# Storing the first row of the first tile by itself in a DMA-bound rotary-embedding kernel

## The chip, the cores and the metric

The kernel runs on 1 core of one Trainium2 chip. The metric is device time of one execution in microseconds (us). A profile covers one execution; its span is about 1.4 us shorter than the measured time of that execution. Only executions that were classed as fast enter comparisons.

## The reference, cut to what matters

```python
batch, seq, dim, num_heads = 16, 512, 1024, 16           # head_dim 64, half 32
x = x.reshape(batch, seq, num_heads, head_dim)
x1, x2 = x[..., :half_dim], x[..., half_dim:]
rotated = np.concatenate([x1 * cos - x2 * sin, x1 * sin + x2 * cos], axis=-1)   # float32
```

The input is 33.5 MB and so is the output, each moved once.

## The kernel before

Each of 128 partitions holds several sequence positions, called rows; a row is 1024 floats, 4 KB. A tile is one batch with 4 rows per partition (the first two and the last two tiles, 2 MB) or two batches with 8 rows (six tiles, 4 MB). Tiles are computed in place in a ring of 40 rows per partition: the first six loads fit at once, the last four wait until earlier tiles have been stored.

```python
RING = 5 * R2                     # R1 = 4, R2 = 8
LAG = 10                          # rows of work between a slot's last sum and the refill's issue
...
def stores_of(k):                 # stores that must land before slot k is loaded again
    return sum(b * R1 // R2 == k for b, _ in tiles)
...
def on_sync(sp):                  # all stores, queue q1
    for u in range(NU):
        t, r, k = where(u)
        if r == tiles[t][1] - 1:                      # last row of tile t is summed
            wait_added(sp, u)
            k = u // R2
            sp.dma_start(in_dram(o1, o2, t), in_sbuf(t)).then_inc(...)
...
# ScalarE: all loads, queue q10, and one kind of eviction, in one program order
for u in range(NU):
    if PE2[u]:
        ae.wait_ge(sem_e, n_pe[u])
        ae.activation(xs[:, u % RING, :], t1_ps[:, u % NT1, :], COPY).then_inc(sem_a, 1)
    for t in later.get(u, ()):
        ae.wait_ge(sem_out[k], 16 * stores_of(k))     # stands still until the stores have landed
        load(ae, t)
```

For each row GpSimd multiplies by the sine table, VectorE by the cosine table, and the two products are added by VectorE or by TensorE with ScalarE.

## Time and profile before

| | before |
|---|---|
| time, median of the first 3 runs | 161.40 us (161.40 to 161.44) |
| span of the profile | 159.8 us |
| bytes moved by DMA, mean rate | 67.26 MB, 421 GB/s |
| GpSimd, VectorE busy | 85%, 82% |
| load queue q10 + store queue q1, share of 16 engines | 49.8% + 48.8% |
| first store issued, last store issued, last store landed | 20.2, 151.1, 159.7 us |

How to read it: a share of a DMA queue is the time its packets took, divided by sixteen engines times the span. As both queues together take 98.6%, the sixteen DMA engines are the resource that is full.

### The profile page before, as it was taken

Reading aid. Unit: us, or ns where it says so; the run is one execution under the profiler, and the core shown is the slowest. Engines: PE = TensorE matmul, PEld = TensorE weight load, DVE = VectorE, ACT = ScalarE, POOL = GpSimd, SP = SyncE. Lnnn points to the kernel's source line nnn. Section 1 sums busy time; section 2 is a strip of 40 time slices with the busy share of each in tenths; the row PEclk is TensorE's granted clock in tenths of the full one; section 3 lists DMA queues with packets and bytes.
Section 4 is the critical chain, followed back from the end, with each engine's and each line's share of the span. In section 5 each row is a group of like instructions: output and inputs, shape, how many; then the busy total and the mean of one; then the engine's idle time right before and its main releaser. Section 6 shows DMA issues by size and latency. Waiting matters only on the chain.

```text
span 159.8 us, 568 instructions
## 1 busy us (share of the span) xinstructions
PE 70.9 (44%) x94; PEld 23.3 (15%) x94; DVE 130.6 (82%) x117; ACT 23.9 (15%) x26; POOL 136.4 (85%) x67
## 2 busy tenths in 40 slices
PE   6050005375437642680943409435848764950000
PEld 1020002021202210220211002110222121310000
DVE  0069998799999999987989729899989998989500
ACT  0320000205020502022012020222022202130000
POOL 5069999999999999999999999994999999289400
PEclk9999999959876995576598775995555555576555
DMA  5999999999999999999999999999999999999997
GB/s 144 395 458 480 394 394 431 422 509 410 394 427 427 494 418 402 451 459 404 402 468 443 394 459 451 402 435 418 418 439 472 435 402 418 492 402 435 390 447 304
DMA packets 3170, 67.26 MB, mean 421 GB/s; under 512 B 352, under 2 KB 608, under 8 KB 608
## 3 DMA queue, kind: packets, MB, share of 16 engines
q10 hardware_dynamic: 1728, 33.69, 49.8%
q1 hardware_dynamic: 1440, 33.56, 48.8%
q14 instruction: 2, 0.02, 0.0%
HBM read 33.69 MB, written 33.55 MB: 421 GB/s over the span
## 4 chain that ended last, share of the span: by engine, by line
DMA 30%; POOL 18%; issue 17%; DVE 17%; PE 8%; ACT 3%; ACTq 2%; POOLq 0%; DVEq 0%; SPq 0%
DMA out_dram<-x_sb 18%; POOL t_sb L265 18%; DMA x_sb<-in_x_dram 11%; DVE x_sb L312 8%; PE t_ps L220 8%; DVE t_ps L301 7%; ACT x_sb L186 3%; ACTq L153 1%; DVE t_sb L294 1%; ACTq L174 1%; POOLq L144 0%; POOLq L146 0%; DVEq L311 0%; DVEq L146 0%; SPq L137 0%
## 5 line engine op out<-in xcount | busy, mean ns | idle before, releaser
L265 POOL TENSOR_TENSOR t_sb<-x_sb,s_sb 128x1024 f32<-128x1024 f32 x58 | 134.1, 2363 | 12.5 <-ACT s_sb L178 6.5
L220 PE MATMUL t_ps<-t_sb,ident 128*128 128x512 f32 x84 | 66.1, 940 | 64.8 <-DVE t_ps L301 34.7
L301 DVE TENSOR_TENSOR t_ps<-x_sb,pair_ps 128x1024 f32<-128x1024 f32 x48 | 57.7, 1223 | 8.2 <-ACT x_sb L186 7.9
L312 DVE TENSOR_TENSOR x_sb<-t_ps,t_sb 128x1024 f32<-128x1024 f32 x43 | 52.4, 1220 | 2.7 <-POOL t_sb L265 2.6
L186 ACT ACTIVATE x_sb<-t_ps 128x1024 f32<-128x1024 f32 x21 | 21.5, 1023 | 109.8 <-PE t_ps L220 97.7
L220 PEld LDWEIGHTS t_ps<-t_sb,ident 128*128 128x128 f32 x84 | 21.4, 279 | 109.2 <-DVE t_ps L301 60.2
L301 DVE TENSOR_TENSOR t_ps<-x_sb,tab_ps 128x1024 f32<-128x1024 f32 x16 | 19.3, 1222 | 1.1 <-DMA x_sb<-in_x_dram 0.6
L294 DVE TENSOR_TENSOR t_sb<-x_sb,tab_ps 128x1024 f32<-128x1024 f32 x6 | 7.3, 1215 | 0.0
L272 DVE COPY tab_ps<-stage 128x128 f32<-128x128 f32 x1 | 0.3, 295 | 7.6 <-DMA stage<-in_cos_dram 7.6
L203 PE MATMUL pair_ps<-stage,pick 128*128 128x256 f32 x4 | 2.0, 668 | 5.1 <-DMA stage<-in_sin_dram 5.1
L196 PE MATMUL t_ps<-zero 128*128 128x512 bf16 x6 | 2.7, 630 | 1.3 <-DVE zero L270 1.3
L177 ACT ACT_TABLE_LOAD x1 | 1.3, 1283 | 5.4 <-issue 5.4
L203 PEld LDWEIGHTS pair_ps<-stage,pick 128*128 128x128 f32 x4 | 1.2, 326 | 6.1 <-issue 6.0
L246 POOL TENSOR_SCALAR_AFFINE_SELECT pick<-pick 128x128 f32<-128x128 f32 x2 | 1.4, 704 | 0.1
L196 PEld LDWEIGHTS t_ps<-zero 128*128 128x128 bf16 x6 | 0.7, 137 | 2.4 <-DVE zero L270 1.2
L270 DVE MEMSET zero<- 128x256 uint32 x1 | 0.3, 272 | 0.9 <-PEq L345 0.9
L177 ACT ACTIVATE s_sb<-stage 128x128 f32<-128x128 f32 x1 | 0.3, 310 | 2.3 <-DMA stage<-in_sin_dram 2.3
L181 ACT ACTIVATE s_sb<-pair_ps 128x256 f32<-128x256 f32 x1 | 0.4, 384 | 1.7 <-PE pair_ps L203 1.7
L231 POOL MEMSET ident<- 128x128 f32 x1 | 0.2, 205 | 0.3 <-POOLq L345 0.3
L182 ACT ACTIVATE s_sb<-pair_ps 128x256 f32<-128x256 f32 x1 | 0.4, 378 | 0.0
L233 POOL TENSOR_SCALAR_AFFINE_SELECT ident<-ident 128x128 f32<-128x128 f32 x1 | 0.3, 294 | 0.1
L345 POOL MEMSET const-float32-0.0<- 128x1 f32 x1 | 0.1, 98 | 0.3 <-issue 0.3
(7 smaller groups left out, 1.3 us busy)
## 6 DMA issues: line engine op xcount, KB each, us to landing
x_sb<-in_x_dram ACTq DMA_DIRECT2D x6, 4096.0 KB, 38.8
out_dram<-x_sb SPq DMA_DIRECT2D x6, 4096.0 KB, 25.7
x_sb<-in_x_dram ACTq DMA_DIRECT2D x4, 2048.0 KB, 22.7
out_dram<-x_sb SPq DMA_DIRECT2D x4, 2048.0 KB, 15.0
stage<-in_cos_dram ACTq DMA_DIRECT2D x1, 64.0 KB, 7.5
stage<-in_sin_dram ACTq DMA_DIRECT2D x1, 64.0 KB, 7.3
```

The costliest lines, as they stand in the source:

```text
L153: eng.dma_start(in_sbuf(t), in_dram(x1, x2, t)).then_inc(sem_in[t], 16)
L174: ae.dma_start(stage[:, i, :], table.rearrange("(s r) d -> s (r d)", r=R1)).then_inc(sem, 16)
L177: ae.activation(s1_sb[:, :, 0, :], sv, COPY, scale=-1.0)
L186: ae.activation(xs[:, u % RING, :], t1_ps[:, u % NT1, :], COPY).then_inc(sem_a, 1)
L196: pe.matmul(t1_ps[:, k, b * BANK:(b + 1) * BANK], zero[:, 0:P], zero[:], start=True, stop=True).then_inc(sem_w, 1)
L203: pe.matmul(pair_ps[:, k].rearrange("p c r d -> p (c r d)"), pick[:, k].rearrange("q s b -> q (s b)"), stage[:].rearrange("q c f -> q (c f)"),
L220: ins = pe.matmul(t1_ps[:, u % NT1, b * BANK:(b + 1) * BANK], ident[:], t2[:, b * BANK:(b + 1) * BANK], start=False, stop=True, skip_group ...
L246: pl.affine_select(out=pick[:, k], in_=pick[:, k], compare_op=mybir.AluOpType.is_equal, fill=0.0, base=-k, pattern=[[-2, P // 2], [0, 2]], ...
L265: pl.tensor_tensor(t2_sb[:, u % NT2, :, :, :], swapped(k), over_heads(s_of(t, r)), mult).then_inc(sem_p, 1)
L294: ve.tensor_tensor(t2_sb[:, u % NT2, :, :, :], swapped(k), over_heads(v_ps), mult)
L301: ve.tensor_tensor(t1_ps[:, u % NT1, :].rearrange("p (h d) -> p h d", d=HALF), x_sb[:, k, :, :, :].rearrange("p h t d -> p (h t) d"), c_of ...
L312: ve.tensor_tensor(xs[:, k, :], t1_ps[:, u % NT1, :], t2_sb[:, u % NT2, :, :, :].rearrange("p h t d -> p (h t d)"), add,).then_inc(sem_v, 1)
```

## The change

The intent is to let the store queue start some 7 us earlier: row 0 of the first tile is stored alone when it is summed, rows 1 to 3 follow in one transfer.

```diff
-        def in_dram(single, pairs, t):
+        def in_dram(single, pairs, t, r=0):
             b, n = tiles[t]
-            return single[b] if n == R1 else pairs[:, b:b + 2, :]
+            return single[b, :, r * dim:] if n == R1 else pairs[:, b:b + 2, :]
 ...                                             (in_sbuf likewise)
-            return sum(b * R1 // R2 == k for b, _ in tiles)
+            return (k == 0) + sum(b * R1 // R2 == k for b, _ in tiles)
 ...
+                if u == 0:
+                    wait_added(sp, u)
+                    sp.dma_start(o1[0, :, 0:dim], xs[:, 0, :]).then_inc(sem_out[0], 16)
                 if r == tiles[t][1] - 1:
                     wait_added(sp, u)
                     k = u // R2
-                    sp.dma_start(in_dram(o1, o2, t), in_sbuf(t)).then_inc(...)
+                    sp.dma_start(in_dram(o1, o2, t, t == 0), in_sbuf(t, t == 0)).then_inc(...)
```

More of the change, by code (lines that the diff above doesn't have):

```diff
@@ L111, in bass_split_heads_rope_kernel, with in_sbuf @@
         xs = x_sb[:].rearrange("p n h t d -> p n (h t d)")
-        def in_dram(single, pairs, t):
+        def in_dram(single, pairs, t, r=0):
             b, n = tiles[t]
-            return single[b] if n == R1 else pairs[:, b:b + 2, :]
-        def in_sbuf(t):
+            return single[b, :, r * dim:] if n == R1 else pairs[:, b:b + 2, :]
+        def in_sbuf(t, r=0):
             b, n = tiles[t]
             k = b * R1 % RING
-            return x_sb[:, k:k + n].rearrange("p n h t d -> p (n h t d)")
+            return x_sb[:, k + r:k + n].rearrange("p n h t d -> p (n h t d)")
         def where(u):
@@ L160, in on_sync @@
                     k = u // R2
-                    sp.dma_start(in_dram(o1, o2, t), in_sbuf(t)).then_inc(sem_out[k] if k < EARLY else sem_rest, 16)
+                    sp.dma_start(in_dram(o1, o2, t, t == 0), in_sbuf(t, t == 0)).then_inc(sem_out[k] if k < EARLY else sem_rest, 16)
             sp.wait_ge(sem_rest, 16 * sum(stores_of(k) for k in range(EARLY, NU // R2)))
```

## The prediction

> **What bounds the kernel now.** I read the strip of 40 slices on the profile page first, because it shows every engine and the transfers side by side; then the transfers by stage; then single stretches of two microseconds.
>
> ```profile
> DVE  0069998799999999987989729899989998989500
> POOL 5069999999999999999999999994999999289400
> DMA  5999999999999999999999999999999999999997
> DMA packets 3170, 67.26 MB, mean 421 GB/s; under 512 B 352, under 2 KB 608, under 8 KB 608
> q10 hardware_dynamic: 1728, 33.69, 49.8%
> q1 hardware_dynamic: 1440, 33.56, 48.8%
> ```
>
> GpSimd is 85% busy and VectorE 82%, with gaps near the end. The DMA row has none: 9 in every slice but the first and the last. Queue q10 carries the loads (issued by ScalarE), q1 the stores (issued by SyncE); together they take 98.6% of sixteen engines over the whole span. The next view divides the span into stretches; its last two columns are the DMA share and GB/s.
>
> ```profile
> 0.00:4.00 4.00, 2.74 (x6) 0.73 (x6) 0.27 (x1) 0.00 (x0) 2.33 (x9) 1.00 0.54 143
> 4.00:24.00 20.00, 2.05 (x4) 1.18 (x4) 14.64 (x14) 2.45 (x5) 14.44 (x7) 1.00 1.00 424
> 24.00:140.00 116.00, 64.07 (x82) 20.94 (x83) 106.26 (x95) 20.28 (x20) 110.41 (x48) 0.70 1.01 434
> 140.00:158.00 18.00, 2.05 (x3) 0.44 (x2) 9.43 (x8) 1.20 (x2) 9.27 (x4) 0.59 0.98 421
> 158.00:160.00 2.00, 0.00 (x0) 0.00 (x0) 0.00 (x0) 0.00 (x0) 0.00 (x0) 0.50 0.33 139
> ```
>
> Loads alone (4 to 24 us) move at 424 GB/s, loads and stores mixed at 434, stores alone (140 to 158 us) at 421. All three have full engines. The kernel is therefore a start of some 2.5 us without data, 67 MB at about 430 GB/s (156 us), and a tail of about 1 us: 159.8 us of span, 161.4 us measured.
>
> The chain that ended last seems to contradict this, since its last pieces before the final store are computation:
>
> ```profile
> 142.77 6.97 POOL t_sb L265 x3
> 149.75 0.03 issue
> 149.77 0.02 DVEq L311
> 149.79 0.04 issue
> 149.84 1.23 DVE x_sb L312
> ```
>
> The final store is issued at 151.14 and lands 8.6 us later. But the queue listing of 140 to 158 us has q1 alone at 98.0% of all engines: the store issued before it, at 143.14, lands only 11.8 us later, at 154.9. The final store waits in its queue for some 3.8 us and then takes 2.10 MB / 0.43 MB per us = 4.9 us: 159.8. So computation has about 3.8 us of slack at the end, and the transfers set it.
>
> **What the skill says.** "DMA: Bandwidth & Descriptors", section "Queues, rings and completion order", says that an engine goes round-robin between the queues that have work for it, a packet at a time. The trace agrees. In the two microseconds from 38 to 40 the listing by queue (packets, MB, share) is
>
> ```profile
> q10 hardware_dynamic: 16, 0.52, 60.6%
> q1 hardware_dynamic: 16, 0.26, 30.6%
> ```
>
> that is, each of 16 engines serves one load packet and one store packet in turn, although one is twice as large. The durations come out of it: 0.606 x 32 us / 16 = 1.21 us for the 32 KB row group of a load, 0.306 x 32 / 16 = 0.61 us for the 16 KB of a store. The same page, "Specifications", gives a fabric ceiling of 435 GB/s; the mixed stretch reaches 434. "Perfetto Trace Analysis", section "DMA Optimizations", says that splitting a DMA may finish the task sooner "If DMA engines are generally idle". That condition doesn't hold here: 98.6% busy. This is the heart of my prediction.
>
> **The change part by part.** On the compute engines nothing moves: the comparison of the instruction streams shows the same instructions in the same order on all but SyncE, which issues 11 stores in place of 10. The bytes stay.
>
> Moved: row 0 is summed at 12.01 + 1.23 = 13.24 us (the first 1.23 us addition on VectorE). Its store of 0.52 MB can be issued at about 13.3 us, where the first store was issued at 20.18. Until then only loads are in flight, and they fill the engines (97.9% for q10 from 13 to 24 us). So the early store takes its time from loads; it fills no hole.
>
> Added: each transfer of 128 partitions is 8 packets per engine (16 in 38 to 40 us belong to 16 engines; 1280 data packets in ten stores). The split makes 8 packets more per engine. From 1.21 us for 32 KB and 0.61 us for 16 KB, a packet costs 0.0375 us per KB and about 0.01 us of its own. A 4 KB packet is thus about 0.16 us and a 12 KB packet 0.46, together 0.62 against 0.61: 8 x 0.01 = 0.08 us in all, an estimate. The extra issue on SyncE (0.34 to 0.6 us) is beside everything.
>
> Turned round: because turns are taken by packet, not by byte, the split store loses its head start. In the kernel before, the first store packets run from about 24 us, 3.8 us after the issue, and 8 x (1.21 + 0.61) = 14.6 us later, at 38.4, the first tile has landed (issue 20.18, 18.2 us to landing). In the changed kernel the first packets run from about 13.3 + 3.8 = 17.1; the single row needs 8 x (1.21 + 0.16) = 11.0 us, to 28; the three rows, which queue behind it, 8 x (1.21 + 0.46) = 13.4, to 41.5. So the tile is complete about 3 us **later**. The next stores follow in the same queue: the second tile at about 56 where it was 52.9, the third at about 76 where it was 72.7. What stores lose, loads gain: every load from the fifth on should land 2 to 3 us earlier, the last of them at about 137.5 where GpSimd got it at 140.4.
>
> GpSimd waits for loads only twice, 5.8 us in sum, at 111.3 (2.2 us) and 140.4 (3.6 us). With loads 3 us sooner the first wait vanishes and the second ends at 137.5; the final store is then issued at about 148, not 151.1. That buys nothing: the stores before it still hold the engines until 154.9, and the bytes are the same.
>
> **The sum.** Extra packets +0.08 us. The faster mixed stretch starts 7 us earlier: 7 x (434 - 424)/434 = -0.16. The slower stretch of stores alone starts about 3 us earlier: 3 x (434 - 421)/434 = +0.09. Together 0.0: **161.4 us**.
>
> **The rivals.**
> First, the chain is right and computation sets the end. Then a last load 3 us sooner would take up to 3 us off: 158.4 us, near 2% faster. For it: the chain's own words, and the last store issued 0.04 us after its sum. Against it: q1 at 98.0% from 140 to 158. I give it 3% in any part.
> Second, small packets or a second transfer are dear. If a 4 KB packet took as long as a 16 KB one, 8 x 0.45 = 3.6 us would be added: 165 us. Against it: 32 KB and 16 KB stand at nearly 2 to 1, which leaves 0.01 us for a fixed part; but no large group of 4 KB packets is in this trace. I give a visible loss (over 0.5 us) 6%.
> Third, a refill stalls. The seventh load needs the first two tiles stored, now counted by three transfers. It was issued at 52.9, as soon as the second tile had landed (30.37 + 22.5), while the sixth landed only at 72.7. An issue at 56 still leaves over 16 us of queued loads. The eighth waits for the third tile, issued 72.8, behind a load that lands at 91.9: 76 is in time. If one did run dry, stores would use the engines meanwhile, so even that costs little. 2%.
>
> **Range and chances.** The three runs before lie within 0.04 us. The terms above are each below 0.2 us, and where the order of packets falls differently at the end, an engine more or less in the last microsecond can move some tenths. I take 161.0 to 161.9. Faster by over 2% would need 158.2, below what the bytes allow; slower by over 2% needs 164.6, which only the second rival reaches.
>
> **What would show it right or wrong.** Right: stores-queue packets 1440 + 128 + 16 = 1584; DMA row still without holes; q10 and q1 still about 98.6% in sum; first single-row store issued at 13.3 and 12 to 15 us to landing; the second store (three rows) issued at 20.2 with about 21 us to landing, not 18.2; GpSimd's wait for loads falling from 5.8 us to 3 or less; last store issued near 148 and taking 11 to 12 us to land. Wrong: a final store that lands within 9 us of an earlier issue and a shorter span (computation was the bound); a fuller q1 share at equal bytes (small packets are dear); a slice below 9 in the DMA row after the third (a stall).

## The result, and the profile after

| | before | changed |
|---|---|---|
| median of 6 runs | 161.38 us (161.27 to 161.44) | 162.19 us (161.76 to 162.42) |
| ratio of the fast runs | | 1.0049, interval 1.0035 to 1.0064 |

A ratio is the mean time of one kernel's fast runs over that of the other's fast runs of the same rounds, so it isn't quite the ratio of the two medians. The change costs 0.8 us, outside the predicted range of 161.0 to 161.9, and the changed kernel scatters over 0.66 us where the one before scatters over 0.17. The profile fell on its fastest execution (161.76 us, span 160.3).

From the page of the changed kernel, the DMA row of the 40 slices, the packet total and the two queues:

```profile
DMA  5999999999999999999999999999998999999895
DMA packets 3314, 67.26 MB, mean 419 GB/s; under 512 B 368, under 2 KB 624, under 8 KB 752
q10 hardware_dynamic: 1728, 33.69, 49.7%
q1 hardware_dynamic: 1584, 33.56, 48.7%
```

The bytes are the same, and q1 has the 1584 packets foretold. The DMA row has two slices at 8 (near 122 and 150 us), which the prediction had named as a sign of a stall; the packet records show that from 9 us to the first engine's end all sixteen engines had a packet throughout, so these are not holes. The transfers by stage, with the DMA share and GB/s as the last two columns:

```profile
4.00:24.00 20.00, 2.04 (x4) 1.17 (x4) 14.63 (x14) 2.45 (x5) 14.43 (x7) 1.00 1.02 434
24.00:140.00 116.00, 64.61 (x80) 20.52 (x80) 104.88 (x95) 19.46 (x19) 111.90 (x49) 0.68 1.00 431
140.00:158.00 18.00, 3.02 (x5) 1.05 (x4) 10.35 (x10) 2.05 (x2) 7.84 (x4) 0.59 0.99 425
```

The engines are as full in each stage as before, and the rates are as near to 430 GB/s (434, 431 and 425 for 424, 434 and 421). The two stores of the first tile (KB, us from issue to landing):

```profile
out_dram<-x_sb SPq DMA_DIRECT2D x1, 1536.0 KB, 21.5
out_dram<-x_sb SPq DMA_DIRECT2D x1, 512.0 KB, 14.7
```

The row was issued at 13.28 us and took 14.7; the three rows, issued at 20.20, took 21.5 and landed at 41.7, where the whole tile had landed at 38.4. The head start was lost to the turns, as foretold. Waits of the kernel before (us in total, times, longest):

```profile
ACT x_sb L186 <- issue: 8.7, 1, 8.7
DVE t_ps L301 <- ACT x_sb L186: 8.3, 9, 3.8
POOL t_sb L265 <- DMA x_sb<-in_x_dram: 5.8, 2, 3.6
ACT x_sb L186 <- DMA out_dram<-x_sb: 3.4, 1, 3.4
```

and of the changed one:

```profile
ACT x_sb L190 <- DMA out_dram<-x_sb: 15.6, 3, 6.4
DVE t_ps L305 <- ACT x_sb L190: 10.5, 9, 3.4
POOL t_sb L269 <- DMA x_sb<-in_x_dram: 1.6, 1, 1.6
```

GpSimd's wait for loads fell as foretold. But ScalarE, which issues the refills, stood still for 15.6 us until stores had landed (before, 3.4 us, or 12.1 if the 8.7 us that the page puts under "issue", which end just after two refills are issued at 92.18 us, are counted too), and VectorE paid 2.2 us more for ScalarE's evictions. So the last store was issued hardly earlier:

```profile
150.90 0.34 SPq L165 DMA_DIRECT2D out_dram<-x_sb  x1
```

Where, then, are the 0.56 us by which this profile's span is longer (160.34 for 159.78)? In its last microsecond. Each of the 16 engines ends its part of a transfer with a packet of 4 bytes, counted under "under 512 B". The queue listing of before, from 158 to 159.4 us and from 159.4 on:

```profile
DMA packets 33, 0.28 MB, mean 199 GB/s; under 512 B 16, under 2 KB 16, under 8 KB 16
DMA packets 0, 0.00 MB, mean 0 GB/s; under 512 B 0, under 2 KB 0, under 8 KB 0
```

All 16 final packets lie in the first window. The changed kernel, same windows:

```profile
DMA packets 31, 0.28 MB, mean 199 GB/s; under 512 B 14, under 2 KB 14, under 8 KB 14
DMA packets 2, 0.00 MB, mean 0 GB/s; under 512 B 2, under 2 KB 2, under 8 KB 2
```

Fourteen engines were done by then, two were not. Sorted by time, the packet records give the sixteen last of these 4-byte packets. The records name no engine; as q1 has 16 such packets for each of its transfers (160 before, 176 after), I take them as one of each engine. On the clock of the windows, the **mean** of the 16 engines is 158.95 us before and 158.95 in the changed kernel: on average the transfers ended no later. The **last** engine is at 159.35 before and 159.98 after, 1.03 us behind the mean where it had been 0.40. The span ends 0.35 to 0.50 us after the last engine in all these profiles.

### The profile page after: what moved, and what is told of

Its sections match the earlier page's. It is cut to its first block, busy times and chain, and to the rows that moved or that the text cites. A ratio compares the mean times of both kernels' runs of the same rounds, so it can differ in the third digit from the quotient of the medians.

```text
span 160.3 us, 569 instructions
## 1 busy us (share of the span) xinstructions
PE 72.4 (45%) x94; PEld 23.5 (15%) x94; DVE 130.1 (81%) x117; ACT 24.0 (15%) x26; POOL 136.5 (85%) x67
## 3 DMA queue, kind: packets, MB, share of 16 engines
q1 hardware_dynamic: 1584, 33.56, 48.7%
## 4 chain that ended last, share of the span: by engine, by line
DMA 31%; DVE 16%; PE 16%; POOL 13%; issue 12%; ACT 3%; ACTq 2%; POOLq 0%; DVEq 0%; SPq 0%
DMA out_dram<-x_sb 19%; PE t_ps L224 16%; POOL t_sb L269 13%; DMA x_sb<-in_x_dram 11%; DVE t_ps L305 7%; DVE x_sb L316 7%; ACT x_sb L190 3%; DVE t_sb L298 2%; ACTq L153 1%; ACTq L178 1%; DVEq L315 0%; POOLq L144 0%; POOLq L146 0%; DVEq L302 0%; SPq L137 0%
## 5 line engine op out<-in xcount | busy, mean ns | idle before, releaser
L224 PE MATMUL t_ps<-t_sb,ident 128*128 128x512 f32 x84 | 67.6, 956 | 64.3 <-DVE t_ps L305 39.4
L190 ACT ACTIVATE x_sb<-t_ps 128x1024 f32<-128x1024 f32 x21 | 21.5, 1024 | 110.7 <-PE t_ps L224 95.1
## 6 DMA issues: line engine op xcount, KB each, us to landing
out_dram<-x_sb SPq DMA_DIRECT2D x1, 1536.0 KB, 21.5
out_dram<-x_sb SPq DMA_DIRECT2D x1, 512.0 KB, 14.7
```

The costliest lines, as they stand in the source:

```text
L224: ins = pe.matmul(t1_ps[:, u % NT1, b * BANK:(b + 1) * BANK], ident[:], t2[:, b * BANK:(b + 1) * BANK], start=False, stop=True, skip_group ...
```

## The experiments

Two theories after the result. **S**: no DMA engine runs dry, but one of the sixteen ends late. **C**: computation, held up by ScalarE's waits, issues the last stores too late, so that the store queue runs dry. A third, **F**, holds that the extra transfer and packets cost by themselves. This table is for all profiles, sorted by what they show; the single runs follow. "Idle" is time in which engines had no packet, from the packet records, as a mean over the engines from 9 us to the first engine's end; ends are those of the final 4-byte packets, on the clock of the windows. Medians are of the fast runs, of which there are six but for c11 (four timed), c6 and c9 (five) and d3 (three).

| kernel | median us | ratio (95%) | idle us | mean end | last end | last - mean |
|---|---|---|---|---|---|---|
| before | 161.38 | 1 | 0.0 | 158.95 | 159.35 | 0.40 |
| c6 before, LAG 12 | 161.35 | 1.0001 (0.994 to 1.007) | 0.0 | 158.99 | 159.34 | 0.35 |
| c7 first tile whole, one row later | 161.38 | 0.9981 (0.994 to 1.002) | 0.0 | 158.98 | 159.45 | 0.47 |
| c8 last tile split 1+3 | 161.38 | 0.9982 (0.994 to 1.003) | 0.0 | 159.00 | 159.52 | 0.52 |
| c5 2+2 rows, LAG 12 | 161.43 | 0.9990 (0.995 to 1.004) | 0.0 | 158.98 | 159.46 | 0.48 |
| d1 row 0 at row 1, LAG 12 | 161.58 | 1.0007 (0.998 to 1.003) | 0.0 | 159.02 | 159.65 | 0.63 |
| the change | 162.19 | 1.0049 (1.004 to 1.006) | 0.0 | 158.95 | 159.98 | 1.03 |
| c1 the change again | 162.13 | 1.0051 (1.003 to 1.007) | 0.0 | 159.02 | 160.45 | 1.43 |
| c3 the change, LAG 12 | 161.88 | 1.0043 (1.003 to 1.006) | 0.0 | 159.07 | 160.06 | 1.00 |
| d4 c3 again | 161.94 | 1.0017 (0.999 to 1.005) | 0.0 | 159.08 | 160.74 | 1.66 |
| d2 3+1 rows, LAG 12 | 162.06 | 1.0036 (1.001 to 1.006) | 0.0 | 159.02 | 160.19 | 1.17 |
| c2 split, both at row 3 | 164.74 | 1.0182 (1.014 to 1.023) | 0.1 | 159.53 | 163.11 | 3.59 |
| c4 2+2 rows | 161.91 | 1.0036 (1.002 to 1.005) | 0.5 | 159.59 | 159.72 | 0.14 |
| c10 row 0 at row 1 | 161.84 | 1.0036 (1.002 to 1.006) | 0.6 | 159.74 | 160.25 | 0.50 |
| c9 3+1 rows | 163.38 | 1.0103 (1.006 to 1.014) | 0.9 | 160.08 | 160.30 | 0.22 |
| c11 second tile split 1+3 | 163.56 | 1.0133 (1.012 to 1.015) | 2.4 | 162.32 | 162.72 | 0.40 |
| c12 first tile whole, four rows later | 164.20 | 1.0187 (1.016 to 1.022) | 1.4 | 161.64 | 163.54 | 1.89 |
| d3 second tile split, LAG 12 | 163.44 | 1.0096 (1.004 to 1.015) | (profile slow, not used) | | | |

In the rounds of c5 to c8 one run of before at 163.53 us counted as fast, which pulls those ratios down; the medians of the fast runs (161.35 to 161.43 against 161.32) differ by 0.11 us at most.

In the eleven profiles from before down to d2, none with idle time, the mean end lies between 158.95 and 159.08 us, and what differs is the last engine. For the change, c1, c3 and d4 the span is 0.56, 1.03, 0.64 and 1.32 us longer than that of before, and the last engine is 0.63, 1.03, 0.60 and 1.26 us further behind the mean than in before.

### c1: the change again

No edit.

> The changed kernel once more, unaltered, for the spread of its executions and a second profile. The first result was 162.19 us (161.76 to 162.42) and its profile fell on the fastest execution. All theories: 161.8 to 162.5, ratio 1.003 to 1.006. Theory S (the 16 DMA engines never run dry but end further apart): in the last microseconds nearly all engines have posted their last semaphore packet by 159.5 us and one to three come 0.5 to 1.5 us later, with the last store issued no later than 151.2. Theory C (computation: stores land 3 us later, ScalarE stands still before its loads for 15.6 us instead of 12.1, and the last store comes too late in the slow executions): last store issued at 151.5 to 153 and a hole in the store queue before it.

Ratio 1.0051: the loss repeats. Theory C's hole isn't there (idle 0.0), theory S's late engine is, larger. The same two windows of the queue listing as above, for c1:

```profile
DMA packets 36, 0.34 MB, mean 246 GB/s; under 512 B 15, under 2 KB 15, under 8 KB 15
DMA packets 2, 0.02 MB, mean 4 GB/s; under 512 B 1, under 2 KB 1, under 8 KB 1
```

Fifteen engines end in the first window, one after it, at 160.45 us. In this profile that engine can be followed, since a packet starts where the one before it on its engine ended, and the records can be chained. At the load that lands near 50 us it is level with the median engine (another one is 0.41 us behind there); it is 0.83 behind from 69 us on, 0.89 at 122 and 1.61 from 137 us to the end. So it falls behind in two places. In the first, the listing from 55.8 to 56.6 us shows an instruction fetch on the same engine (packets, MB, share):

```profile
q14 instruction: 1, 0.01, 2.4%
```

which is one 8 KB packet, 0.024 x 16 x 0.8 = 0.31 us long, and the window from 56.1 to 56.2 us a single 32 KB load packet beside it:

```profile
q10 hardware_dynamic: 1, 0.03, 108.8%
```

1.088 x 16 x 0.1 = 1.74 us instead of 1.21. Together these are the 0.83 us. The fetch comes in every profile, before included, and the packet behind the one near 56 us is 0.34 to 0.53 us too long in each of the eleven without idle time. The second place is the window from 125.95 to 126.00 us, which has one packet of each queue:

```profile
q1 hardware_dynamic: 1, 0.03, 219.2%
q10 hardware_dynamic: 1, 0.02, 76.4%
```

The store packet took 2.192 x 16 x 0.05 = 1.75 us instead of 1.21, while the load packet of another engine took its regular 0.61. Between 120 and 130 us the packets of this profile exceed their regular durations by 0.81 us in sum, those of before by 0.10. That sum alone is no cause: it is 0.75 us in c8 and 0.83 in c5, which lost nothing. But by the same chaining no engine of theirs has more than 0.22 and 0.44 us of it; here one has 0.71. One of c1's six executions took only 161.36 us, so the loss is not in every execution, and a profile shows a single one.

### c2: the split without the earliness

```diff
-                if u == 0:
+                if u == 3:
```

> The split without the earliness: row 0 is stored by itself but only when row 3 is summed, so both stores are issued at about 20.2 us. Theory F (a further transfer and 128 small packets cost by themselves): as slow as the change, ratio 1.004 to 1.006. If the earliness is what costs (loads and stores taking turns from 17 us on, while the first loads are still needed), 161.2 to 161.6, ratio 0.999 to 1.001. By the turns of packets, the first tile lands still later than in the change: 24 + 11.0 + 13.4 = 48 us, the second at 63, and ScalarE stands still longer before its loads; theory C then expects more loss than in the change, 163 or more.

The worst loss of the first four, 1.0182. The expected late landings came (first tile near 48 us, second at 63), but the engines stood idle for only 0.1 us and the mean engine ended at 159.53, 0.6 us later than in before. In the two windows at the end:

```profile
DMA packets 34, 0.34 MB, mean 246 GB/s; under 512 B 13, under 2 KB 13, under 8 KB 13
DMA packets 12, 0.13 MB, mean 28 GB/s; under 512 B 4, under 2 KB 4, under 8 KB 4
```

Four engines end after 159.4 us, the last of them at 163.11: of the 3.7 us by which the span is longer than before, 3.2 are this tail. From 68.40 to 68.45 us there is one store packet:

```profile
q1 hardware_dynamic: 1, 0.03, 302.6%
```

3.026 x 16 x 0.05 = 2.42 us, twice its regular 1.21. My expectation for an innocent late split (0.999 to 1.001) was wrong, and so was theory C's reason for a loss.

### c3 and d4: the change with LAG 12

```diff
-    LAG = 10
+    LAG = 12
```

> The change with LAG 12 for 10: ScalarE issues each late load two rows of work later (some 4.6 us), so that it no longer stands still for store landings that came 3 us later. Theory C: the loss goes away, 161.2 to 161.6, ratio 0.999 to 1.001, ScalarE's wait for stores falls from 15.6 us to under 8, and the last store is issued at 148 to 150. Theory S: the time stays at 161.8 to 162.5, although the last store is issued earlier.

> The change with LAG 12 again, unaltered. The first time 1.0043 with no idle engines and a last engine 1.0 us behind the mean. All theories: 1.003 to 1.006; if the late engine were chance from run to run, this could come out at 1.000 to 1.002 too.

c3 took 161.88 us, 1.0043, with the last store issued at 148.9 instead of 150.9 and ScalarE's wait for stores at 8.1 us instead of 15.6. Earlier computation did not bring the time back, so theory C does not explain the change. d4, the same kernel, gave 1.0017 with an interval that includes 1 (its runs of before scattered up to 162.39); its median, 161.94, repeats c3's 161.88 (one of its six runs took 161.17), and its profile has the last engine 1.66 us behind the mean.

### c6: before with LAG 12

The same edit on the kernel before.

> The kernel before with LAG 12 for 10, the control for the run with LAG 12 on the change. ScalarE should stand still less and the last store be issued some us earlier. Transfers bound: 161.0 to 161.5, ratio 0.998 to 1.001. If computation had a part in the end: 160 or less.

161.35 us against 161.32 for the fast runs. ScalarE has no wait for stores left in its list, but the last store is issued at 151.11 us (151.14 in before) and not some us earlier, as I had expected. LAG by itself changes nothing in the time that these runs show.

### c7: the lag of the stores without the split

```diff
-                    wait_added(sp, u)
+                    wait_added(sp, u + (t == 0))
```

> The kernel before, with no split and no small packet, but the store of the first tile waits for one row more (row 4, about 22.5 us for 20.2). Every store then lands 2 to 3 us later and the loads run ahead, as in the change, with the packets of before. If it is the lag of the stores behind the loads that puts the engines out of step: 161.7 to 162.5, ratio 1.003 to 1.007. If it is the small packets: 161.1 to 161.5, ratio 0.999 to 1.001, and the engines' last packets lie within 0.9 us as before.

161.38 us, no loss, though the stores lag and the loads lead as in the change (mean end of the loads at 137.0 us; 136.4 in the change, 139.5 before). The shift of stores against loads alone isn't the cause.

### c8: the same split on the last tile

```diff
-                if u == 0:
+                if u == NU - R1:
```

> The same split at the other end: row 0 of the last tile alone, the other three rows in one transfer, nothing at the start. Same number of packets as the change. Theory F (packets and transfers cost by themselves): ratio 1.004 to 1.006. Theory S (the engines must have time to drift apart after the stores are shifted): 161.1 to 161.5, ratio 0.999 to 1.002. In neither is there a gain, as the store queue is already full at the end.

(The other lines of the split are moved to the last tile likewise.) 161.38 us, no loss with the same number of packets and transfers: theory F falls.

### c4 and c5: two rows and two rows

```diff
-                if u == 0:
+                if u == 1:
...                                   (rows 0 and 1, then rows 2 and 3; c5 with LAG 12 as well)
```

> Two rows and two rows instead of one and three: packets of 8 and 8 KB, first store issued at about 15.5 us. Turns: 8 x (1.21 + 0.31) = 12.2 us for each half, from about 19.3, so the first tile is complete near 43.7, the second near 58. Theory C expects a little more loss than in the change (stores land 2 us later still): 162.3 to 163. Theory S expects a time between that of before and the change, or at its spread: 161.4 to 162.4, not ordered by the landing of the stores. Theory F: equal to the change, since the number of packets is equal.

> Two rows and two rows, with LAG 12. The run of 2 and 2 rows had all engines end within 0.3 us, but its last store was issued only at 154.1 and all engines stood idle for some 0.4 us in the last slices. With LAG 12 the last store should come near 149 to 151 and the idle time go. If holes cost there and the engines stay in step: 161.0 to 161.4, ratio 0.998 to 1.001. If the idle time was what had brought the engines back into step (theory S): the spread comes back and the time stays at 161.7 to 162.4.

c4 lost 0.4% in another way: its last store was issued only at 153.8 us, the engines were idle for 0.5 us, and after the idle time they ended in step (last engine 0.14 us behind the mean). That is theory C, in a neighbour of the change. With LAG 12 the last store was issued at 147.8 us, the idle time went, the late engine did not come back, and the loss was gone (161.43 us). An early start (at about 15.5 us), an added transfer and as many added packets are all present in c5, so none of them has to cost anything. Its packets are of 8 KB, though, not of 4 and 12.

### c9, c10, c11 and the same with LAG 12: other places for the split

c9 stores three rows when row 2 is summed and then one; c10 is the change with `if u == 1`; c11 splits the second tile with `if u == R1`. d1 to d3 repeat them with LAG 12.

> Three rows early (issued at about 17.9 us) and one row after: packets of 12 KB and then of 4 KB. Turns: 21.7 + 13.4 + 11.0 = 46 us for the first tile, the second near 61. If small packets beside the loads are what puts one engine behind: as the change or worse, ratio 1.004 to 1.018. If the loss belongs to an early start of the stores: less than the change, ratio below 1.003, since the start is 2 us earlier than before instead of 7.

> The change, but row 0 alone is stored when row 1 is summed (about 15.5 us for 13.3). It lies between the change (ratio 1.005) and the late split (1.018). If the loss grows steadily with the lag of the stores: ratio 1.006 to 1.012. If it is a matter of how the turns happen to fall (which packet of one engine meets what at about 56 and 125 us): anything from 0.999 to 1.010, out of order.

> The same split on the second tile: row 0 of it alone at about 22.5 us, when the store queue is busy with the first tile, so that nothing starts earlier; the other three rows follow. Eight turns more, as in the change: the second tile lands at 38.4 + 11.0 + 13.4 = 63 us for 52.9. If small packets beside 32 KB loads do it: ratio 1.004 to 1.018, and one engine ends over 1 us behind the median one. If the early start does it: 0.999 to 1.002.

> Row 0 alone stored at about 15.5 us, LAG 12. Without LAG 12 the ratio was 1.0036 with 0.6 us of idle engines near 140 us and all engines ending within 0.6 us. If the single-row packets put one engine behind: last engine 1 us or more behind the mean, ratio 1.003 to 1.008, as in the change. If it is how turns happen to fall: 0.999 to 1.003 is as likely. Idle engines near 140 us: none, in both.

> Three rows and then one, LAG 12. Without it the ratio was 1.010 with 0.85 us of idle engines, the last store issued at 154. If the idle time was all of the loss: 0.999 to 1.002. If single-row packets put one engine behind: 1.003 to 1.008 and a last engine 1 us behind the mean.

> The second tile split 1 and 3, LAG 12. Without it the ratio was 1.013 with 2.4 us of idle engines. The second tile lands at 62 in this kernel, when the first five loads of 4 MB or less are nearly through, so the load queue still starts again late: slow packets at 66 to 80 us remain in any case. If the idle time was most of the loss: 1.000 to 1.006. If the lag of one engine is: 1.008 or more.

All three without LAG 12 lost time to idle engines. The plainest is c11; its DMA row is

```profile
DMA  5999999999999989999999999999999999599997
```

and the two stretches from 136 to 144 us read

```profile
136.00:140.00 4.00, 3.53 (x4) 1.18 (x4) 4.00 (x5) 0.00 (x0) 4.00 (x3) 0.50 0.83 356
140.00:144.00 4.00, 1.62 (x3) 0.84 (x3) 3.59 (x4) 1.02 (x1) 4.00 (x2) 0.50 0.67 287
```

The share drops to 0.83 and 0.67: the loads were through early, the store queue ran dry and waited for the next sum. In c9 the last store was issued 3 us later than before:

```profile
154.13 0.34 SPq L165 DMA_DIRECT2D out_dram<-x_sb  x1
```

With LAG 12 the ratios fell from 1.0036 to 1.0007 (c10, d1), from 1.0103 to 1.0036 (c9, d2) and from 1.0133 to 1.0096 (c11, d3; the intervals overlap). What remains in d2 goes with a last engine 1.17 us behind the mean. d1 matters most: it is the change with row 0 issued 2 us later, has the same 4 KB packets beside the loads, and has a last engine only 0.63 us behind and no clear loss. So small packets need not put an engine behind; my reading after the first eight runs, that they do, does not hold as it stood. But this is the profile of d1's fastest run, and the intervals of d1 and d4 overlap. Every profile without idle time whose last engine is 1 us or more behind has 4 KB packets beside the loads, so that they have a part in it is not excluded.

### c12: the first tile whole, held back four rows

```diff
-                    wait_added(sp, u)
+                    wait_added(sp, u + 4 * (t == 0))
```

> The kernel before, unsplit, with the store of the first tile held back to row 7 (about 29.3 us): the first tile lands near 48 and the second near 62, as in the late split, with no small packet. If the loss of the late split (ratio 1.018, one engine 4 us behind) comes from loads that are issued too late because the second tile lands at 62: ratio 1.01 to 1.02. If it comes from the small packets: 0.999 to 1.003.

1.0187, as bad as c2, without any split. The second tile lands near 62 us, the refill that waits for it is issued when the loads queued before are through, and a string of packets between 66 and 80 us takes longer than regular (21 us in sum, about 1.3 us per engine; 0.75 us in sum in before), besides 1.4 us idle and a late engine. The packet records of c12, c2 and c11 alike have no load packet in flight from 62.5 to 66.8 us; stores alone are on the engines. So a load queue that starts again late goes with the loss, and c2 and c11, whose second tile lands as late, aren't clean tests of the split.

No variant beat the kernel before; c5, c6, c7 and c8 equal it.

## Why the prediction was right or wrong

**What bounds it: right.** The mean engine ended at 158.95 us, as before; the time is made of transfers.

**Turns by packet: right, within 1.1 us.** Row 0 issued at 13.28 (13.3 foretold), 14.7 us to landing (12 to 15); three rows 21.5 us (about 21); the second tile issued at 30.65 and landed 25.6 later, at 56.3 (56); GpSimd got the last load at 138.6 (137.5).

**Cost of the packets: right.** c8 carries the same additional packets and c5 as many of them, at no measurable cost.

**The last store near 148 us, 11 to 12 us to land: wrong.** It was issued at 150.90 and took 9.4. The step let loads arrive earlier without asking what the later stores would hold up: ScalarE stands still in front of its refills, and VectorE behind ScalarE. It cost the change itself nothing that c3 could win back.

**The sum, 0.0 us: wrong, and this is the step that failed.** It summed the work of an average engine, and for that engine it was right. The exactness is in part luck: the mixed stretch ran at 431 GB/s and the stores alone at 425, where the sum had taken 434 and 421. The prediction had the missing term in one clause, "an engine more or less in the last microsecond can move some tenths", and sized it at tenths. Measured, the last engine went from 0.40 us behind the mean to between 1.00 and 1.66 in the four profiles of the split at row 0 (the change, c1, c3, d4), and that carries the loss.

**The rivals.** Computation at the end is not the cause of the change's loss (c3), but the "3.8 us of slack" was thinner than I took it for: c4, c9, c10 and c11, with turns or issues a little later, ran the store queue dry. Dear small packets: not by themselves (c8). A refill that stalls: not in the change, but "even that costs little" was wrong, as c12 lost 1.9%.

**What stays open.** That the loss of the change is the late end of one engine is shown by its end times, without idle time, beside an unchanged mean. In c1 that engine lost its time around 56 us, where the instruction fetch lies, and around 122 to 126 us, to slow store packets. Both kinds occur in kernels without loss too (near 56 us one engine of before loses 0.66 us). Why the packets were slow, why both kinds met on one engine of c1, and why the split at row 0 brings this about where d1 and c5 do not, no run shows. A collision in memory of an engine that is out of step with the others is conceivable; it was not tested.

## What to carry to other kernels

When DMA queues are full from start to end, starting one transfer earlier only reorders bytes, and as queues take turns by packet, cutting a transfer into more and smaller packets can make it land later than if it had started late and whole. Judge such a kernel by the end of its last DMA engine and not by the mean share: a microsecond can go to one engine out of sixteen that the busy figures do not show. Before delaying any store, ask which refill waits for it and what else stands in that engine's program behind the refill.

## What the Trainium skill lacked or had wrong

- "DMA: Bandwidth & Descriptors", section "Queues, rings and completion order": it says that an engine switches queues by packet, and the trace agrees (16 and 16 packets in turn, 1.21 and 0.61 us each). It gives a typical packet as several descriptors; here a turn was one packet of up to 32 KB, one partition's part of a transfer, and the trace does not show its descriptors. It lacks the consequence for split stores: a tile whose first part started 6.9 us earlier landed 3.3 us later.
- The same page, section "iDMA fabric", has in passing, in an explanation that it marks as unconfirmed, that "a bulk load runs at the pace of its slowest engine". The trace agrees for a whole kernel (means of 158.95 and 158.95 us, last engines at 159.35 and 159.98), but no page gives how far the last engine falls behind the mean (0.14 to 3.6 us here) or how to see it.
- No page gives the cost of an instruction fetch to running transfers: in c1 one 8 KB packet of 0.31 us beside a 32 KB packet that took 1.74 us for 1.21.
- "Perfetto Trace Analysis", section "DMA Optimizations", names idle engines as the case for splitting a DMA. No run here tests that case. The page lacks the other side: with engines full, splits cost from nothing (c5, c8) over 0.5% (the change) to 1.8% (c2, whose loads also start again late).
